# The FFN of a hybrid diffusion step in scaled float16 pairs, split once and kept in DRAM

## The chip, the cores and the metric

The kernel runs on one core of one Trainium2 chip. A core has a matrix engine (TensorE, "PE" in the profile), a vector engine (DVE), a scalar engine (ACT), a third compute engine (POOL) and an engine that only issues transfers (SP). Each has its own queue of instructions and works through it in order; semaphores tie them together. [...] Transfers between DRAM and SBUF run on 16 DMA engines, which all queues share.

The metric is the device time of one execution in microseconds (us), given as the median over several runs.

## What is computed

One layer of a backbone over 128 context tokens and 1024 latent tokens, 1152 rows in all, with a model width of 1024. Attention heads and mLSTM heads stand side by side, one output projection merges them, and an FFN follows. What matters here is the FFN:

```python
def swiglu(h, w_gu, w_down):
    g, u = jnp.split(h @ w_gu, 2, axis=-1)
    return (jax.nn.silu(g) * u) @ w_down

def trunk_layer(...):
    ...
    mix = jnp.concatenate([attn_o, hm], axis=-1) @ w_out
    x = x + g1 * mix
    h2 = rmsnorm(x, norm2_w) * (1 + sc2) + sh2
    x = x + g2 * swiglu(h2, w_gu, w_down)
    return x, ak, av, st_f, st_b
```

All tensors are float32. `w_gu` is 1024 x 5632 (gate, then up, `D_FF` = 2816 columns each), `w_down` is 2816 x 1024.

## The kernel before

**Products of pairs.** To keep the accuracy of float32, each operand is split into a high part and the rest ("hi" and "lo"), and three products are added in PSUM: hi x hi, hi x lo, lo x hi. The projections at the start (`Scaled`, `linear_tok`, `head_project`) use float16 pairs: the weights are measured first (a sum of absolute values by ACT, a maximum over partitions, `power_scale`), then scaled by a power of two. The FFN and the output projection use pairs of the type fp32r, which need no scale.

**Stages in order of time.** Modulation vectors and the first norm come first. Then the four mLSTM heads: while the projection of head h+1 runs on TensorE (`head_project`), the scan of head h (`head_mlstm`) and the rest of the modulation (`ada_rest`) are woven in by `weave` and `beside`, which hand out steps of a side job in a given ratio to steps of the main one. The query projection follows, then attention and the output projection of the first third of the rows, and then the FFN.

**FFN.** The 1152 rows are cut into three chunks of 384 (`CT`). For a chunk, `norm2` makes the normed and modulated rows, transposed, as a pair of tiles (`a_tiles`). The 22 tiles of `D_FF` (`NF`) are worked in five groups (`GROUPS`, in the last chunk `LAST`) of 4 or 5. For a tile, `gate_up` loads a piece of 1024 x 128 weights for gate and one for up, and `products` (lines 1271 to 1273) issues 3 x 8 matmuls with 384 columns into each of two PSUM banks; then tanh, two DVE steps and a split give the activations as a pair. After a group, `down` multiplies its tiles with pieces of `w_down` for each half of the output: `three_blocks` (lines 1090 to 1092) works with row block 0 and then with blocks 1 and 2, and `add_gated` (lines 1079 and 1080) adds the gated result to the residual rows. The very last group goes through `down_last` (lines 1356 to 1358). So the residual rows are read and written once per group.

**Loading weights.** `load_piece` serves both the FFN and the output projection: SP issues one load of 0.5 MB into one of two `raw` buffers (line 151), ACT casts the high part (line 152), and DVE (every third time) or POOL subtracts for the low part (line 135). High and low parts have five buffers each. Every chunk loads and splits all of `w_gu` and `w_down` again.

**What runs beside the FFN.** The attention of the next chunk is woven into the groups of the current one, with a transfer that transposes on SP for each half of the probabilities (lines 1009 and 1010); the output projection of the next chunk, `attn_out`, stands before the last group, and its `norm2` is woven into the down product of that group. `finish` writes the rows of the chunk before. The order that the engines' queues finally get is that of a scheduler, which starts from this text and the priorities given with `hot`.

**Buffers.** PSUM has four banks with the tag `mm` for all these products. The tiles with the tags `b0` to `b5` in the pool `hp` are large and shared over time: `b3` to `b5` hold the normed input during the heads; `b0` and `b1` take the key stacks when attention begins; `b2` and `b3` are the pair of tiles that the FFN reads.

## Time and profile before

| | us |
|---|---|
| median of 3 runs | 1625.24 |
| lowest and highest of them | 1623.43, 1627.29 |
| span of the profiled execution | 1626.0 |

The profile is one execution, seen by the hardware profiler. Its page gives the span from the first to the last instruction; the profiled execution has no other time of its own, and its span lies within the range of the runs. Rows of the page's parts and of the trace's views have these forms:

- Groups of instructions: line, engine, operation, output and inputs by their names in the program, shapes, count, then busy us in all and the mean of one in ns, then the idle time just before them and what ended most of it.
- Stages: start and end in us, the length, then busy us with the count of instructions for PE, weight loads (PEld), DVE, ACT and POOL, the granted clock of TensorE as a share of full speed, the mean busy share of the DMA engines, and GB/s. Asked for one line alone, the row has only the busy time of that line's engine.
- Timeline: start in us, duration in us, engine, line, operation, and in brackets the idle time before and what ended it.

Matmuls are pipelined: the duration of one row is longer than the step from one start to the next, so the pace of TensorE is read from the starts.

### The profile page before, as it was taken

The page shows a single profiled execution, that of the slowest core. Times are in us where ns is not written, and L with a number is a line of the kernel's source. Part 1 is how long each engine was busy: PE and PEld are TensorE (multiplying, and loading weights), DVE is VectorE, ACT ScalarE, POOL GpSimd, SP SyncE. Part 2 cuts the span into 40 slices and gives each one's busy share as a digit, 9 for nine tenths or more (in the row PEclk, how much of TensorE's full clock was granted, in tenths as well). Part 3 has the DMA queues.
Part 4 walks back from the last instruction along what each step waited for, and adds up shares of the span by engine and source line. Part 5 has one row for each costly group of instructions (what it writes and reads, how often), then busy time and mean ns, then how long its engine had stood idle before and what let it go on. Part 6 is the DMA issues. An engine that isn't in the chain of part 4 may idle for free. (4 is left out here: it accounts for less than half of the span.)

```text
span 1626.0 us, 23528 instructions
## 1 busy us (share of the span) xinstructions
PE 1517.4 (93%) x8688; PEld 1258.8 (77%) x8688; DVE 970.8 (60%) x2059; ACT 732.5 (45%) x1251; POOL 606.5 (37%) x387
## 2 busy tenths in 40 slices
PE   5899899899879768999999999999999999999996
PEld 2745566575557557998989899898898989899995
DVE  3843364958987665467672646777674474432445
ACT  3744252434544554545643344565562453333332
POOL 0411020404344514443435354444344444545443
PEclk8999999999999878999999999999999999999998
DMA  9355352201156855767873546777684445545441
GB/s 357 94 165 130 101 147 58 84 21 46 41 198 147 195 107 112 168 168 174 187 184 112 149 141 219 187 184 173 156 183 128 134 142 170 152 126 149 130 142 66
DMA packets 386313, 232.73 MB, mean 143 GB/s; under 512 B 169910, under 2 KB 346502, under 8 KB 386198
## 3 DMA queue, kind: packets, MB, share of 16 engines
q1 hardware_dynamic: 384342, 228.04, 52.7%
q10 hardware_dynamic: 1856, 3.19, 0.6%
q8 instruction: 68, 1.11, 0.3%
q14 instruction: 47, 0.39, 0.1%
HBM read 181.16 MB, written 11.69 MB: 119 GB/s over the span
## 5 line engine op out<-in xcount | busy, mean ns | idle before, releaser
L135 POOL TENSOR_TENSOR wlo<-raw,whi 128x1024 fp32r<-128x1024 f32 x146 | 357.8, 2454 | 445.7 <-ACT whi L152 407.9
L152 ACT CAST whi<-raw 128x1024 fp32r<-128x1024 f32 x219 | 224.4, 1025 | 375.9 <-DMA raw<-in_w_gu_dram 137.8
L1272 PE MATMUL mm<-aTl,whi 128*128 128x384 f32 (+2 forms) x1088 | 364.7, 335 | 0.7 <-POOL aTl L135 0.7
L1273 PE MATMUL mm<-aTh,wlo 128*128 128x384 f32 (+2 forms) x1088 | 364.4, 335 | 0.0
L1271 PE MATMUL mm<-aTh,whi 128*128 128x384 f32 (+2 forms) x1088 | 363.4, 336 | 0.7 <-DVE tn L1299 0.7
L1272 PEld LDWEIGHTS mm<-aTl,whi 128*128 128x128 f32 x1088 | 205.9, 189 | 1.7 <-POOL aTl L135 0.9
L1271 PEld LDWEIGHTS mm<-aTh,whi 128*128 128x128 f32 x1088 | 205.4, 189 | 2.0 <-DVE tn L1299 1.3
L1273 PEld LDWEIGHTS mm<-aTh,wlo 128*128 128x128 f32 x1088 | 205.8, 189 | 0.1
L135 DVE TENSOR_TENSOR wlo<-raw,whi 128x1024 fp32r<-128x1024 f32 (+1 forms) x73 | 88.1, 1206 | 142.2 <-ACT whi L152 141.7
L1090 PE MATMUL mm<-whi,hl 128*128 128x512 f32 x372 | 145.8, 397 | 1.5 <-ACT hl L1303 1.4
L1091 PE MATMUL mm<-wlo,hl 128*128 128x512 f32 x372 | 146.9, 397 | 0.0
L1092 PE MATMUL mm<-whi,hl 128*128 128x512 f32 x372 | 144.3, 396 | 0.7 <-POOL hl L135 0.7
L1007 DVE SCALAR_TENSOR_TENSOR pl<-pr,st,ph 128x1152 f16<-128x1152 f32 (+1 forms) x72 | 107.8, 1498 | 39.4 <-ACT ph L1006 39.4
L488 PE MATMUL wi<-ipair,hT 128*128 128x384 f16 (+2 forms) x392 | 128.2, 327 | 2.8 <-ACT ipair L216 2.8
L489 PE MATMUL wi<-ipair,hT 128*128 128x384 f16 (+2 forms) x392 | 128.1, 327 | 0.0
L490 PE MATMUL wi<-ipair,hT 128*128 128x384 f16 (+2 forms) x392 | 127.1, 326 | 0.0
L135 POOL TENSOR_TENSOR hl<-tn,hl 128x384 fp32r<-128x384 f32 x66 | 84.2, 1276 | 105.0 <-ACT hl L1303 105.0
L1003 ACT ACTIVATE pr<-S,st 128x1152 f32<-128x1152 f32 (+1 forms) x72 | 81.1, 1127 | 89.1 <-DVE st L1002 86.1
L1299 DVE SCALAR_TENSOR_TENSOR tn<-tn,mm 128x384 f32<-128x384 f32 (+2 forms) x68 | 36.7, 540 | 137.9 <-PE mm L1273 97.5
L1080 DVE TENSOR_TENSOR x<-x,t 128x512 f32<-128x512 f32 x102 | 116.5, 1163 | 0.8
L1000 PE MATMUL S<-kst,qT 128*128 128x384 f32 (+1 forms) x400 | 88.3, 355 | 19.6 <-ACT pr L1003 19.2
L1002 DVE TENSOR_REDUCE st<-S 128x1 f32<-128x1152 f32 (+1 forms) x72 | 88.9, 1234 | 18.3 <-PE S L1000 17.8
(353 smaller groups left out, 2684.6 us busy)
## 6 DMA issues: line engine op xcount, KB each, us to landing
raw<-in_w_gu_dram SPq DMA_DIRECT2D x132, 512.0 KB
raw<-in_w_down_dram SPq DMA_DIRECT2D x60, 512.0 KB
a<-in_w_ada_dram SPq DMA_DIRECT2D x32, 512.0 KB
gl<-g_d SPq DMA_DIRECT2D x36, 256.0 KB
aw<-in_w_ada_dram SPq DMA_DIRECT2D x16, 512.0 KB
iraw<-in_w_in_dram SPq DMA_DIRECT2D x32, 256.0 KB
raw<-in_w_out_dram SPq DMA_DIRECT2D x15, 512.0 KB
x<-in_x_sample_dram SPq DMA_DIRECT2D x13, 512.0 KB
```

The source lines that it names most:

```text
L135: (dve if eng == "dve" else pool).tensor_tensor(out=out, in0=full, in1=hi, op=ALU.subtract)
L152: nc.scalar.copy(hi[:, :n], raw[:, :n])
L488: mm(ps[:, :n], ah, wh[:, k % 2, c0 : c0 + n], start=(k == 0), stop=False)
L489: mm(ps[:, :n], ah, wl[:, k % 2, c0 : c0 + n], start=False, stop=False)
L490: mm(ps[:, :n], al, wh[:, k % 2, c0 : c0 + n], start=False, stop=(k == KD - 1))
L1080: eng.tensor_tensor(out=x1[:, cs], in0=x1[:, cs], in1=t, op=ALU.add)
L1090: mm(ps, ah, wh[:, k % 2, :], start=(k == 0), stop=False)
L1091: mm(ps, ah, wl[:, k % 2, :], start=False, stop=False)
L1092: mm(ps, al, wh[:, k % 2, :], start=False, stop=(k == nk - 1))
L1271: mm(ps, wh[:, k, :], th[:, k, :], start=(k == 0), stop=False)
L1272: mm(ps, wh[:, k, :], tl[:, k, :], start=False, stop=False)
L1273: mm(ps, wl[:, k, :], th[:, k, :], start=False, stop=(k == KD - 1))
```

## The change

The FFN's operands become float16 pairs with scales, and the weights are split only in the first chunk. In parts:

1. **Measurement of weights** (`measure`). Beside heads 1 to 3 and the query projection, all of `w_gu` and `w_down` is loaded in 33 units of 1 MB into buffers with the tags `b0` to `b2`. ACT squares them with a column sum into `sq`, for 55 tiles of weights. One matmul with ones adds over the partitions, and DVE makes a power-of-two scale and its inverse for each tile (`wsc`, and `fsc` for the activations). Each load follows a small POOL copy that reads a tile which the heads have just made.
2. **Bound on the normed rows** (`bound_h2`). From the modulation vectors, a power-of-two scale that is put into them.
3. **Pairs** (`split_pair`, `gu_piece`, `down_piece`). In chunk 0 a piece is loaded, scaled and split: on odd turns with one ACT and one DVE step, on even turns with two ACT steps and one on POOL. The pair is one tile and is written to DRAM (`gu_d`, `wd_d`). In chunks 1 and 2 a piece is one load of that pair. The pairs take buffers of either of the two old tags in turn, ten in all.
4. **Activations.** `gate_up` keeps them in float32 in one of 20 slots; ACT takes a sum of absolute values of each tile. When a group is done, `rescale` finds the maximum of these sums, makes a power of two, and scales and splits the group's tiles. The inverse scale goes into `add_gated`.
5. **Groups.** Two in a chunk (12 and 10 tiles), three in the last (10, 8 and 4). `down` holds three PSUM banks, one for each row block, and uses each piece for all three. The down product of a group stands behind the first three tiles of the next one (for the short last group, behind all of it); that of the last group stands behind the output projection of the next chunk, and `norm2` is woven into it.
6. **Normed rows.** The pair is one float16 tile, `b2` or `b3` in turn.

```diff
-GROUPS = [(0, 4), (4, 4), (8, 4), (12, 5), (17, 5)]
-LAST = [(0, 5), (5, 5), (10, 4), (14, 4), (18, 4)]
+GROUPS = [(0, 12), (12, 10)]
+LAST = [(0, 10), (10, 8), (18, 4)]
...
+    def measure(after):
...
+        def load(u):
+            src, a, _ = srcs[u]
+            t = hp.tile([P, 3072], F32, name=nm("ms"), tag=f"b{u % 3}")
+            pool.tensor_copy(t[:, 0:1], after())
+            dma(t[:, 0:2048].rearrange("p (a n) -> p a n", a=a), src)
+            return t
...
+            if a == 2:
+                act(t[:, 0:2048], t[:, 0:2048], AF.Square, accum_out=sq[:, col : col + 1])
+            else:
+                for i in range(2):
+                    v = t[:, 0:2048].rearrange("p (k i n) -> p i k n", k=KD, i=2)[:, i]
+                    act(v, v, AF.Square, accum_out=sq[:, col + i : col + i + 1])
+            yield
...
+        mm(ps[:, 0:NS], ones, sq, start=True, stop=True)
...
-    weave(head_project(1, sts[1]), beside((scan, 1.15), (ada, 0.45)), 56, 56)
+    weave(head_project(1, sts[1]), beside((scan, 1.15), (ada, 0.45), (meas, 0.2)), 56, 56)
...
-    weave(head_project(2, sts[2]), beside((scan, 1.15), (ada, 0.55)), 56, 56)
+    weave(head_project(2, sts[2]), beside((scan, 1.15), (ada, 0.55), (meas, 0.22)), 56, 56)
...
-    weave(head_project(3, sts[3]), beside((scan, 1.15), (kwork, 0.5)), 56, 56)
+    weave(head_project(3, sts[3]), beside((scan, 1.15), (kwork, 0.5), (chain(bound_h2(), meas), 0.3)), 56, 56)
...
-    weave(linear_tok(w_q, 0, 512, ev_q, QFIRST), scan, 24, 60)
+    weave(linear_tok(w_q, 0, 512, ev_q, QFIRST), beside((scan, 1.0), (meas, 0.15)), 24, 60)
     emit(scan)
+    emit(meas)
...
+    def split_pair(src, shape, col, keep):
+
+        t, (hi, lo) = pair(shape)
+        raw = wp.tile([P, 1024], F32, name=nm("raw"), tag="raw", bufs=2)
+        dma(raw.rearrange("p (a b) -> p a b", b=shape[1]), src)
+        sc = wsc[:, 0, col : col + 1]
+        lo_count[0] += 1
+        if lo_count[0] % 2:
+            act(t[:, 0], raw, AF.Copy, scale=sc)
+            dve.scalar_tensor_tensor(out=t[:, 1], in0=raw, scalar=sc, in1=t[:, 0], op0=ALU.mult, op1=ALU.subtract)
+        else:
+            act(raw, raw, AF.Copy, scale=sc)
+            nc.scalar.copy(t[:, 0], raw)
+            sub(t[:, 1], raw, t[:, 0], "pool")
+        dma(keep, t)
+        return hi, lo
...
-                act(tn[:, cs], g, AF.Tanh, scale=0.5)
+                act(tn[:, cs], gp_, AF.Tanh, scale=fsc[:, 0, f : f + 1])
...
+            jk = ft.tile([P, D], BF16, name=nm("jk"), tag="t2", bufs=3)
+            act(jk[:, 0:CT], tn, AF.Abs, accum_out=g["st"][:, i : i + 1])
...
+        for i, tn in enumerate(g["a"]):
+            hl = hlp.tile([P, 2, CT], F16, name=nm("hl"), tag="hl", bufs=SLOTS)
+            act(hl[:, 0], tn, AF.Copy, scale=m[:, 1:2])
+            dve.scalar_tensor_tensor(out=hl[:, 1], in0=tn, scalar=m[:, 1:2], in1=hl[:, 0], op0=ALU.mult, op1=ALU.subtract)
+            g["hl"].append(hl)
...
+    def down(c, a, g):
+        for n in range(2):
+            gate = gate_bc(1, c, n)
+            banks = [bank() for _ in range(CB)]
+            for j in range(0, g["nf"], 2):
+                w = down_piece(c, (g["f0"] + j) // 2, n)
+                for i, ps in enumerate(banks):
+                    down_products(ps, g, j, i, w)
+                    if j + 2 == g["nf"]:
+                        add_gated(a["x1"][i], ps, gate(c * CB + i), n, inv=g["inv"])
+                    yield 2
...
-    nc = _bacc.Bacc("TRN2", target_bir_lowering=False, num_devices=1)
+    nc = _bacc.Bacc("TRN2", target_bir_lowering=False, num_devices=1, dynamic_dma_scratch_size=1024)
```

[...]

More of the change, by code (lines that the diff above doesn't have):

```diff
@@ L1301, in gate_up @@
[L1301 to L1317 removed]
+                dve.scalar_tensor_tensor(out=tn[:, cs], in0=tn[:, cs], scalar=fsc[:, 1, f : f + 1], in1=gp_, op0=ALU.mult, op1=ALU.mult)
@@ L1332, in finish, with down_last @@
             yield
-    def down_last(c, a, f0, nf):
+    def down_last(c, a, g):
         gs, ws = [], []
@@ L1444, in hybrid_step @@
         else:
-            main = groups(c, cur, LAST[:-1])
+            grps = [new_group(*x) for x in LAST]
+            main = groups(c, cur, grps)
             for _ in range(4):
```

264 lines of the change are left out of this document (183 added, 81 removed).

## The prediction

> **What bounds the kernel now.** I read the page's first two parts first: how busy each engine is, and how that is spread over forty slices of the span.
>
> ```profile
> PE 1517.4 (93%) x8688; PEld 1258.8 (77%) x8688; DVE 970.8 (60%) x2059; ACT 732.5 (45%) x1251; POOL 606.5 (37%) x387
> PEclk8999999999999878999999999999999999999998
> ```
>
> TensorE is busy nearly everywhere, but the page warns that a busy PE is not a PE at its peak, so I went on to the table of stages: columns are PE, weight loads, DVE, ACT, POOL, the granted clock, the DMA share and GB/s.
>
> ```profile
> 0.00:50.00 50.00, 29.33 (x152) 13.67 (x152) 24.39 (x114) 23.85 (x50) 4.19 (x9) 0.86 0.97 342
> 160.00:400.00 240.00, 226.62 (x1522) 150.97 (x1521) 152.32 (x519) 96.67 (x283) 54.27 (x79) 0.98 0.30 76
> 400.00:450.00 50.00, 41.47 (x224) 25.21 (x225) 45.08 (x154) 25.59 (x74) 16.39 (x18) 0.93 0.18 63
> 660.00:850.00 190.00, 188.13 (x1086) 171.35 (x1086) 128.70 (x176) 101.86 (x133) 77.04 (x37) 1.00 0.77 179
> 850.00:985.00 135.00, 135.00 (x704) 123.58 (x703) 63.58 (x103) 51.82 (x70) 62.49 (x32) 1.00 0.47 138
> 985.00:1340.00 355.00, 350.99 (x1943) 320.51 (x1942) 232.42 (x336) 177.78 (x239) 152.10 (x71) 1.00 0.65 167
> 1395.00:1605.00 210.00, 210.00 (x1112) 196.99 (x1112) 80.76 (x94) 66.01 (x84) 99.26 (x51) 1.00 0.45 132
> ```
>
> The rows are: start; mLSTM heads 0 to 3; query projection; chunk 0 with attention beside it; chunk 0 after attention; chunk 1; chunk 2. From 660 us on, PE is idle for 1.9, 0, 4.0 and 0 us, at a clock of 1.00. Whether the busy time is full pace shows in the timeline, between the starts of the first and last row of an unbroken run. The FFN's products first, 384 then 512 columns wide:
>
> ```profile
> 1404.77 0.34 PE L1272 MATMUL mm<-aTl,whi 128*128 128x384 f32 x1
> 1411.88 0.34 PE L1271 MATMUL mm<-aTh,whi 128*128 128x384 f32 x1
> ...
> 1395.76 0.39 PE L1091 MATMUL mm<-wlo,hl 128*128 128x512 f32 x1
> 1399.96 0.39 PE L1091 MATMUL mm<-wlo,hl 128*128 128x512 f32 x1
> ```
>
> The first pair has 41 steps between it: 7.11/41 = 0.1734 us a product. The second has 18: 4.20/18 = 0.2333 us. So the FFN is bound by how many products PE must stream and at what pace. A loader, a wait or an engine that gets cheaper there gives nothing; only the pace does.
>
> **What the change takes away.** The projections before it already use float16 pairs, with the same tiles; their runs give the new pace.
>
> ```profile
> 171.99 0.33 PE L490 MATMUL wi<-ipair,hT 128*128 128x384 f16 x1
> 173.94 0.33 PE L490 MATMUL wi<-ipair,hT 128*128 128x384 f16 x1
> ...
> 439.96 0.38 PE L489 MATMUL mm<-ipair,hT 128*128 128x512 f16 x1
> 444.06 0.38 PE L490 MATMUL mm<-ipair,hT 128*128 128x512 f16 x1
> ```
>
> 12 steps in 1.95 us are 0.1625 us; 19 steps in 4.10 us are 0.2158 us. The counts come from the groups of instructions by form; each of these lines has two sisters with the same count.
>
> ```profile
> L1272 PE MATMUL mm<-aTl,whi 128*128 128x384 f32 x1024 | 345.8, 338 | 0.0
> L1091 PE MATMUL mm<-wlo,hl 128*128 128x512 f32 x372 | 146.9, 397 | 0.0
> L1357 PE MATMUL mm<-wlo,hl 128*128 128x512 f32 x24 | 9.5, 394 | 0.0
> ```
>
> Gate and up: 3 x 1024 = 3072 products x (0.1734 - 0.1625) = 33.5 us. Down: 3 x (372 + 24) = 1188 x (0.2333 - 0.2158) = 20.8 us. Together **-54.3 us**. Regrouping changes no product count. The 192 narrower products of the first two tiles I leave at nothing, either way.
>
> [...]
>
> **What it adds: the measurement beside the heads.** 33 loads of 1 MB, 44 ACT squares of 1024 columns and 11 of 2048, in the stage from 160 to 450 us. Nearest rows for ACT, with the rows of the splitting steps that I need below:
>
> ```profile
> L199 ACT ACTIVATE jk<-iraw 128x1024 bf16<-128x1024 f32 x20 | 21.2, 1058 | 7.6 <-DMA iraw<-in_w_in_dram 7.3 <-issue 0.3
> L199 ACT ACTIVATION_READ_ACCUMULATOR jk<-iraw 128x1 f32 x20 | 3.9, 193 | 0.0
> L216 ACT ACTIVATE ipair<-iraw,isc 128x1024 f16<-128x1024 f32 x10 | 11.5, 1152 | 1.9 <-PE wi L490 1.8
> L219 ACT ACTIVATE iraw<-iraw,isc 128x1024 f32<-128x1024 f32 x10 | 10.9, 1140 | 2.1 <-DVE isc L204 2.1
> L220 ACT CAST ipair<-iraw 128x1024 f16<-128x1024 f32 x10 | 10.4, 1041 | 0.0
> L152 ACT CAST whi<-raw 128x1024 fp32r<-128x1024 f32 x207 | 217.0, 1049 | 348.4 <-DMA raw<-in_w_gu_dram 137.8 <-PE mm L1272 58.4 <-DMA raw<-in_w_down_dram 48.1
> L1303 ACT CAST hl<-tn 128x384 fp32r<-128x384 f32 x66 | 33.7, 510 | 34.2 <-DVE tn L1300 34.0
> ```
>
> 44 x 1.25 + 11 x about 2.2 = 79 us of ACT. ACT has 122 of 290 us there now; it would have 201. Its queue is in order: behind each square wait the head's evacuations, its exponentials and so the matmuls that read them, while PE has only 22 us of slack (290 less 226.62 and 41.47). The loads fit: 34.6 MB at the 342 GB/s of the first row is 101 us, against a share of 0.30 used. But each load is issued by SP behind a small POOL copy that waits for a fresh block of the head, and the next head's weights queue behind it on SP.
>
> No row has a square of this size in this place, so bounds. Below: 0, since nothing of that stage is removed. Above: if the whole stage fell from 94% busy PE (226.62/240) to the 83% of the row from 400 to 450 us (41.47/50), where ACT and DVE are crowded, 290 x 0.11 = 32 us. DVE is not loaded more here, so I take less than half: **+14 us**. The tail of it (one matmul over the column sums, some ten small DVE steps, the bound on h2) is inside that.
>
> **Chunk 0: splitting and keeping.** 66 pieces are loaded, split and also written to DRAM; 4 are needed before 660 us. Besides the ACT rows above:
>
> ```profile
> L135 DVE TENSOR_TENSOR wlo<-raw,whi 128x1024 fp32r<-128x1024 f32 x67 | 83.9, 1252 | 118.0 <-ACT whi L152 117.6 <-issue 0.4
> L217 DVE SCALAR_TENSOR_TENSOR ipair<-iraw,isc,ipair 128x1024 f16<-128x1024 f32 x10 | 16.0, 1612 | 8.6 <-ACT ipair L216 8.6
> L135 POOL TENSOR_TENSOR wlo<-raw,whi 128x1024 fp32r<-128x1024 f32 x140 | 350.1, 2504 | 435.7 <-ACT whi L152 397.8 <-issue 10.8 <-DVE t L1079 8.4
> L135 POOL TENSOR_TENSOR ipair<-iraw,ipair 128x1024 f16<-128x1024 f32 x10 | 23.4, 2348 | 64.7 <-ACT ipair L220 64.7
> ```
>
> A split took 1.05 + 2.50 us (two of three, POOL) or 1.05 + 1.25 us (DVE). Now an odd piece takes 1.15 + 1.61 = 2.8 us, an even one 1.14 + 1.04 + 2.35 = 4.5 us; mean 3.65 against 3.13. The two raw buffers are held from issue to end of split. The landing shows between an issue by SP and the cast that waited for it, quiet and beside attention:
>
> ```profile
> 1404.70 0.37 SPq L151 DMA_DIRECT2D raw<-in_w_gu_dram  x1
> 1409.29 1.05 ACT L152 CAST whi<-raw 128x1024 fp32r<-128x1024 f32 x1 [2.05 <-DMA raw<-in_w_gu_dram]
> ...
> 1001.13 0.81 SPq L151 DMA_DIRECT2D raw<-in_w_gu_dram  x1
> 1007.97 1.05 ACT L152 CAST whi<-raw 128x1024 fp32r<-128x1024 f32 x1 [4.14 <-DMA raw<-in_w_gu_dram]
> ```
>
> Quiet: 4.2 us; beside attention 6.0 us. With 0.4 us of hand-overs the loader makes a piece every (4.2 + 3.65 + 0.4)/2 = 4.1 us, where PE now takes 24 x 0.1625 = 3.9 us for one. Beside attention the write of another piece lies ahead of it, 1.5 us (0.52 MB at 342/0.97 GB/s, first row of the stages): (7.5 + 4.05)/2 = 5.8 us.
>
> How many pieces each stretch split before:
>
> ```profile
> 660.00:850.00 190.00, 38.42 (x37) 1.00 0.77 179
> 850.00:985.00 135.00, 32.94 (x33) 1.00 0.47 138
> ```
>
> That is a piece every 5.1 and 4.1 us. The 70 include four of the output projection and the first of chunk 1; chunk 1 now splits nothing, and ten pieces instead of five may be ready ahead, so some 59 remain: 33 x 5.8 + 26 x 4.1 = 298 us, against 325 - 18 = 307 us that PE needs. The loader just keeps up. DMA is tighter: 0.77 x 190 = 146 us of full work in the first stretch and 33 writes x 1.5 = 50 us more make 196 us, for a stretch that PE would end in about 180: 16 us over, part of which may move into the second stretch (0.47 x 135 = 63 us used). Bounds: 0, if the traffic spreads; 45 us, if a piece takes the loader 1 us more than reckoned in the first stretch (33 us) and nothing is caught up in the second (12 us). Nothing here can gain. I take **+12 us**, near the DMA sum.
>
> [...]
>
> **Groups, rescaling, chunks 1 and 2.** Seven groups instead of fifteen. Each now waits for its own maximum (two PE steps, seven small DVE steps) before 4 to 12 tiles are scaled: ACT 0.51 us each, DVE about 0.6 us (1612 ns x 384/1024), so about 12 us to the last tile. Behind it waits the group's down product; ahead of it in PE's order lie three tiles of the next group (6 x 3.9 = 23 us) or the output projection of the next chunk (72 products x 0.2333 = 17 us). Bounds: 0, and 7 x 2 us where attention delays it. I take **+2 us**. Fewer groups save DVE and POOL work, off PE's path: nothing. In chunks 1 and 2 a piece is one 0.5 MB load without a split; of the 4.0 us of idle PE in chunk 1 and some near its end I let **3 us** go. What is late next there is PE itself.
>
> The sum, against the execution's own span: 1626.0 - 54.3 + 14 + 12 + 2 - 3 = 1596.7. The span is 0.8 us above the median of the runs, 1625.24, so **1596 us**.
>
> **Rivals.**
> - All additions hide: 1626 - 54 - 3 - 1 = 1568. For it: ACT and DMA are half free in the heads, and ten pieces of stock. Against: PE there waits for ACT already.
> - The heads pay in full, 32 instead of 14: 1614, and with 25 us in chunk 0 about 1627, no change.
> - Slower: chunk 0 becomes bound by its DMA. Transposes, writes and reads share SP's queue; if a landing beside attention reaches 11 us, a piece takes (11 + 4.05)/2 = 7.5 us: 33 x 7.5 + 26 x 4.5 = 365 us for PE's 307, 58 in place of 12, so 1642. It decides from 41 us in chunk 0 on (54 + 3 - 14 - 2), a mean of 5.9 us a piece. For it: share 0.77 already. Against: quiet second stretch.
> - The pace does not change, since f32 products as wide were not bound by their type: 1626 + 14 + 12 + 2 - 4 = 1650. The float16 runs speak against it.
> - Products overlap further than the runs show, until the float16 weight load is the bound, at 0.10 us:
>
> ```profile
> L489 PEld LDWEIGHTS <-hT 128*128 128x128 f16 x432 | 43.2, 100 | 31.0 <-issue 8.2
> ```
>
>   then down alone gives 1188 x (0.2333 - 0.10) = 158 us for 21, so 1459. The same runs speak against it, since they have this weight load and step at 0.2158 us. [...]
>
> **Chances.** Mine (1580 to 1618) 0.50; all hidden (1565 to 1580) 0.23; heads in full 0.11 (half of it no change); chunk 0 on DMA 0.13; pace unchanged 0.02; further overlap 0.01. Range 1568 to 1634: it leaves out the worse half of the slower case, the fast edge and the two small ones. A measurement of this kernel tells about 0.2%, 3.3 us, from no change: faster 0.80, same 0.05, slower 0.15.
>
> **What would show it.** Starts of float16 FFN products 0.1625 and 0.2158 us apart; chunk 2, from first gate product to last down product, about 18 us shorter; the heads' stage some 14 us longer with ACT near 70%; PE waits in chunk 0 that lead back to DMA of raw pieces; none in chunk 1. Wrong if the heads grow by over 32 us, chunk 0 by over 40, or a rescale leaves PE idle for more than 2 us.

## The result, and the profile after

The changed kernel takes 1679.74 us (median of 4 runs, 1679.43 to 1680.37) beside 1626.26 us before (4 runs, 1623.43 to 1628.04): a ratio of 1.034, 95% interval 1.0321 to 1.0359. It is slower, where 1596 us and faster were forecast. The profiled execution spans 1677.6 us, 51.6 more than before. The first row of its page:

```profile
PE 1499.1 (89%) x8714; PEld 935.7 (56%) x8714; DVE 871.6 (52%) x2065; ACT 745.6 (44%) x1388; POOL 265.0 (16%) x252
```

TensorE is busy for 18 us less and yet the span is longer: idle time grew by 70 us. Where it lies is seen from the starts of four products in the timeline: the first of the output projection (the heads and query projection are over), and the first gate product of chunks 0, 1 and 2. They divide the spans of all runs of this study as follows (us; the last column runs to the end of the span). The stages are those of one profiled execution each, and the runs of one kernel lie up to 15 us apart (h_ungated), so single differences of a few us carry little weight.

| kernel | time (ratio to before) | span | heads | up to chunk 0 | chunk 0 | chunk 1 | chunk 2 |
|---|---|---|---|---|---|---|---|
| before | 1626.26 | 1626.0 | 457.8 | 622.1 | 361.5 | 351.4 | 291.0 |
| after | 1679.74 (1.034) | 1677.6 | 510.3 | 671.6 | 401.3 | 332.9 | 271.7 |
| h_none | 1619.13 (0.9975) | 1621.4 | 458.8 | 624.1 | 394.4 | 331.4 | 271.5 |
| h_loads | 1633.17 (1.0062) | 1633.2 | 475.4 | 629.9 | 400.0 | 331.8 | 271.4 |
| h_squares | 1648.18 (1.0163) | 1646.1 | 478.4 | 635.5 | 406.9 | 332.3 | 271.4 |
| h_ungated | 1639.46 (1.0098) | 1639.9 | 478.3 | 648.0 | 388.1 | 332.4 | 271.4 |
| h_free | 1638.60 (1.0098) | 1638.3 | 472.2 | 642.6 | 392.1 | 332.3 | 271.2 |
| h_va | 1640.59 (1.0104) | 1637.5 | 482.8 | 643.9 | 390.9 | 331.2 | 271.5 |
| h_kt3 | 1668.15 (1.027) | 1667.0 | 500.1 | 662.1 | 402.0 | 331.3 | 271.6 |
| h_so | 1663.29 (1.0239) | 1660.2 | 492.4 | 659.5 | 397.6 | 331.7 | 271.5 |
| c_late | 1658.01 (1.0204) | 1653.7 | 505.7 | 668.1 | 383.1 | 331.3 | 271.3 |
| c_raw3 | 1653.00 (1.0173) | 1649.6 | 502.9 | 670.9 | 373.4 | 333.2 | 272.1 |
| c_odd | 1646.67 (1.0134) | 1639.4 | 505.5 | 664.6 | 371.5 | 332.0 | 271.4 |
| c_alias | 1642.37 (1.0107) | 1639.6 | 507.0 | 664.8 | 372.1 | 331.0 | 271.7 |
| c_noload | 1606.30 (0.9895) | 1607.5 | 510.6 | 669.7 | 334.9 | 331.7 | 271.3 |
| c_all | 1633.68 (1.0063) | 1634.0 | 504.6 | 670.0 | 359.5 | 333.0 | 271.4 |
| c_all_nostore | 1627.89 (1.0022) | 1620.7 | 506.5 | 669.5 | 347.2 | 332.3 | 271.7 |
| g_best | 1609.01 (0.991) | 1604.5 | 484.1 | 640.4 | 357.8 | 335.1 | 271.2 |
| g_va | 1609.83 (0.9906) | 1611.3 | 486.3 | 644.6 | 362.2 | 333.2 | 271.2 |

After against before: 49.5 us more up to chunk 0, 39.8 more in it, 18.5 and 19.3 less in chunks 1 and 2. With the forecast pace chunk 0 too should have been 18.1 us shorter, so its loss is 57.9. The gain came in full; about twice its size, 49.5 + 57.9 us, was lost in the two places where the change adds work. The table of stages of after (columns as in the prediction) shows what those two have in common:

```profile
150.00:510.00 360.00, 304.21 (x1860) 193.91 (x1857) 207.12 (x730) 191.11 (x480) 82.73 (x131) 0.93 0.60 164
...
671.60:1072.90 401.30, 353.15 (x2029) 220.66 (x2029) 211.31 (x331) 215.54 (x297) 80.20 (x38) 0.94 0.80 220
1073.00:1406.00 333.00, 328.78 (x1928) 204.47 (x1927) 169.19 (x307) 127.06 (x209) 7.05 (x3) 1.00 0.66 172
1406.00:1650.00 244.00, 244.00 (x1395) 136.31 (x1393) 63.48 (x131) 40.38 (x94) 0.00 (x0) 1.00 0.41 136
```

The same heads, and chunk 0, in before:

```profile
150.00:458.00 308.00, 285.41 (x1855) 185.76 (x1854) 208.80 (x705) 128.60 (x369) 74.91 (x99) 0.97 0.29 77
...
622.10:983.60 361.50, 357.00 (x2024) 326.33 (x2022) 212.79 (x319) 172.47 (x230) 152.56 (x75) 0.99 0.63 158
```

For nearly the same number of products TensorE is idle 55.8 us instead of 22.6 in the heads, and busy 19 us longer, at a granted clock of 0.93 instead of 0.97. So 33 us of the 52 are waits, and 19 are longer busy time; the ratio of the two clocks gives some 12 of these 19 (285.41 x 0.97/0.93 - 285.41), the rest stays open. In chunk 0, 48.2 us are idle instead of 4.5, at a granted clock of 0.94 instead of 0.99. Chunks 1 and 2 run at 1.00, chunk 2 without a gap. The starts of the FFN's products there, 39 steps apart in the first pair of rows and 19 in the second:

```profile
1409.78 0.33 PE L1383 MATMUL mm<-h,wpair 128*128 128x384 f16 x1
...
1416.12 0.33 PE L1383 MATMUL mm<-h,wpair 128*128 128x384 f16 x1
...
1617.38 0.38 PE L1449 MATMUL mm<-wpair,hl 128*128 128x512 f16 x1
...
1621.48 0.38 PE L1450 MATMUL mm<-wpair,hl 128*128 128x512 f16 x1
```

6.34/39 = 0.1626 and 4.10/19 = 0.2158 us: the pace is the one forecast.

### The profile page after: what moved, and what is told of

It reads as the page before. It is cut to its first block, busy times and chain, and to the rows that moved or that the text cites. A ratio compares the mean times of both kernels' runs of the same rounds, so it can differ in the third digit from the quotient of the medians.

```text
span 1677.6 us, 23385 instructions
## 1 busy us (share of the span) xinstructions
PE 1499.1 (89%) x8714; PEld 935.7 (56%) x8714; DVE 871.6 (52%) x2065; ACT 745.6 (44%) x1388; POOL 265.0 (16%) x252
## 5 line engine op out<-in xcount | busy, mean ns | idle before, releaser
L1383 PE MATMUL mm<-h,wpair 128*128 128x384 f16 (+2 forms) x1088 | 349.9, 323 | 4.8 <-DVE tn L1414 3.2
L1384 PE MATMUL mm<-h,wpair 128*128 128x384 f16 (+2 forms) x1088 | 350.4, 323 | 0.5 <-POOL h L137 0.5
L1385 PE MATMUL mm<-h,wpair 128*128 128x384 f16 (+2 forms) x1088 | 350.6, 323 | 0.0
L1449 PE MATMUL mm<-wpair,hl 128*128 128x512 f16 x396 | 149.9, 381 | 1.6 <-DVE tn L1413 1.6
L1450 PE MATMUL mm<-wpair,hl 128*128 128x512 f16 x396 | 150.7, 381 | 0.0
L1451 PE MATMUL mm<-wpair,hl 128*128 128x512 f16 x396 | 149.6, 380 | 0.0
L1384 PEld LDWEIGHTS <-wpair 128*128 128x128 f16 x1088 | 107.3, 99 | 71.1 <-issue 6.8
L1385 PEld LDWEIGHTS <-wpair 128*128 128x128 f16 x1088 | 107.2, 99 | 69.6 <-issue 4.9
L1383 PEld LDWEIGHTS <-wpair 128*128 128x128 f16 x1088 | 107.0, 99 | 67.5 <-issue 2.6
L1088 DVE SCALAR_TENSOR_TENSOR pl<-pr,st,ph 128x1152 f16<-128x1152 f32 (+1 forms) x72 | 103.6, 1441 | 52.8 <-ACT ph L1087 52.8
L1081 PE MATMUL S<-kst,qT 128*128 128x384 f32 (+1 forms) x400 | 98.4, 383 | 34.5 <-ACT pr L1084 27.1
L137 POOL TENSOR_TENSOR wpair<-raw,wpair 128x1024 f16<-128x1024 f32 x33 | 72.7, 2202 | 308.0 <-ACT wpair L1342 287.5
L1416 ACT ACTIVATE jk<-tn 128x384 bf16<-128x384 f32 x66 | 34.4, 521 | 158.9 <-DVE tn L1414 111.7
L1081 PEld LDWEIGHTS S<-kst,qT 128*128 128x128 f32 x400 | 76.7, 209 | 45.3 <-ACT pr L1084 34.3
L1087 ACT ACTIVATE ph<-pr,st 128x1152 f16<-128x1152 f32 (+1 forms) x72 | 83.4, 1159 | 30.3 <-issue 11.3
L1105 PE MATMUL po<-phT,vs 128*128 128x256 f16 x292 | 76.8, 294 | 20.6 <-DMA phT<-ph 14.8
```

What stands on the lines that cost most here:

```text
L1081: mm(S[:, n, 0:w], qT[:, h, :], kst[kv][:, t, c0 + n * w : c0 + (n + 1) * w], start=(t == 0), stop=(t == 1))
L1088: dve.scalar_tensor_tensor(out=plv, in0=prv, scalar=st[:, 3:4], in1=phv, op0=ALU.mult, op1=ALU.subtract)
L1383: mm(ps, wh[:, k, :], th[:, k, :], start=(k == 0), stop=False)
L1384: mm(ps, wh[:, k, :], tl[:, k, :], start=False, stop=False)
L1385: mm(ps, wl[:, k, :], th[:, k, :], start=False, stop=(k == KD - 1))
L1449: mm(ps, ah, wh[:, k], start=(j + k == 0), stop=False)
```

## The experiments on the heads

Some names first. SyncE and GpSimd are SP and POOL of the profile. An evacuation copies finished products out of PSUM; ScalarE evacuates a block of a head into `kt`, VectorE into `va`. `dt` and `sd` are later steps of the scan. The gate is the small GpSimd copy ahead of each load of the measurement.

Theory A says that squares at the head of ScalarE's in-order queue wait for loads that were issued late. Its rivals are the traffic of the loads, or SyncE held behind the gates (theory B), and the plain time of the squares on ScalarE (theory C). Theory A came from two views of after. The waits of the heads, ScalarE's first and then TensorE's longest (who waited, for what: us in all, times, longest):

```profile
ACT ms L539 <- DMA ms<-in_w_gu_dram: 61.9, 17, 19.8
ACT ms L535 <- DMA ms<-in_w_down_dram: 31.4, 6, 9.6
...
PE mm L909 <- DVE sd L887: 17.9, 6, 9.9
```

The squares wait 93 us for their loads, at the head of ScalarE's queue. The timeline shows why the loads are late:

```profile
272.03 0.30 POOL L524 COPY ms<-kt 128x1 f32<-128x1 f32 x2 [16.38 <-ACT kt L801]
272.24 0.39 SPq L525 DMA_DIRECT2D ms<-in_w_down_dram  x1
...
283.42 1.91 ACT L535 ACTIVATE ms<-ms 128x2048 f32<-128x2048 f32 x1 [7.22 <-DMA ms<-in_w_down_dram]
...
285.33 0.35 ACT L801 ACTIVATE kt<-wi,isc 128x128 f32<-128x128 f32 x1
285.79 0.18 POOL L524 COPY ms<-kt 128x1 f32<-128x1 f32 x1 [13.46 <-ACT kt L801]
...
289.72 1.12 ACT L885 ACTIVATE dt<-mm,QT 128x128 f32<-128x128 f32 x4
...
290.35 0.94 DVE L887 TENSOR_TENSOR sd<-mm,dt 128x256 f32<-128x256 f32 x2 [9.96 <-ACT dt L885]
290.83 1.23 PE L909 MATMUL mm<-va,sd 128*128 128x129 f32 x4 [9.94 <-DVE sd L887]
```

A square at 283.42 had waited 7.22 us for its load. Behind it stood the evacuation of kt (285.33), for which the gate copy had waited 13.46 us, and behind the gate stands the next load. It is a loop: square, evacuation, gate, load, square. The head's `dt` (289.72) stands in the same queue, and TensorE ends up waiting 9.94 us.

**h_none**: the measurement is left out; the norms are a constant.

```diff
-        ahead = [load(0), load(1)]
...
+        dve.memset(sq, 1.0)
```

> The measurement's loads, its POOL copies and its squares are left out; the column sums are set to 1, so the scales are constants instead of measured ones. The heads' stage (up to the first product of the output projection) took 457.8 us before the change and 510.3 us after. Every theory: with all of it gone the stage ends near 458 to 462, the total near 1679 - 50 = 1630. If the stage stays above 475, the growth is not the measurement's at all.

1619.13 us, ratio 0.9975 (0.9955 to 0.9994). Up to chunk 0 it takes 624.1 us, 2.0 more than before: the 47.5 us above that are the measurement's. Chunk 0 keeps 394.4 us, so most of its loss has another cause.

**h_loads**: loads and gate copies as in after, the squares left out, the norms a constant.

```diff
-            if a == 2:
-                act(t[:, 0:2048], t[:, 0:2048], AF.Square, accum_out=sq[:, col : col + 1])
...
+        dve.memset(sq, 1.0)
```

> The 33 loads of 1 MB and their POOL copies stay, the 55 squares are left out (column sums set to 1). Theory A (a square stands at the head of ACT's queue and waits for a load that was issued late, and the heads' evacuations wait behind it): the stage ends within 10 us of the kernel without any measurement, total near 1632. Theory B (the loads' traffic, or SP held behind the POOL copies): the stage stays near 500, total near 1670.

1633.17 us, ratio 1.0062 (1.0039 to 1.0085). The time is theory A's. The heads, 475.4 us, are 16.6 over h_none and not within 10, but far from theory B's 500; up to chunk 0 it is 629.9, 5.8 over h_none, so part of the work seems only to have moved across the boundary.

**h_squares**: the same 55 squares, on three tiles that are loaded once; 30 loads are left out. The squares write their output to the unused end of the tile, as bfloat16, so that the three tiles stay as loaded.

```diff
-            dma(t[:, 0:2048].rearrange("p (a n) -> p a n", a=a), src)
+            if u < 3:
+                dma(t[:, 0:2048].rearrange("p (a n) -> p a n", a=a), src)
```

> The 55 squares stay, but read three tiles that are loaded once; 30 of the 33 loads are left out, so the scales are wrong. Theory A (waiting on late loads): the stage grows by 5 to 15 us over the kernel without measurement, total near 1640. Theory C (79 us of ACT time in a queue that is nearly the bound): it grows by 40 us or more, total near 1672.

1648.18 us, ratio 1.0163 (1.0131 to 1.0195). The heads grow by 19.6 us over h_none, between theory A's 5 to 15 and theory C's 40; up to chunk 0 it is 635.5 us, 11.4 over h_none. Loads alone and squares alone make 17 us there; together they cost 47.5. By the whole times the sum is less far off: 14.0 and 29.1 us alone, 60.6 together. Some 17 to 30 us exist only when a square can wait for a load, which fits the loop.

**h_ungated**: the gate copy alone is left out.

```diff
-            pool.tensor_copy(t[:, 0:1], after())
```

> All of the measurement stays, only the POOL copy ahead of each load goes, so that a load is issued as soon as its buffer is free. Theory A: squares find their data landed; the stage ends near 475, total near 1645. Theories B and C: no change, total 1675 to 1682.

1639.46 us, ratio 1.0098 (1.0038 to 1.0158): 40 us below after, as theory A expected; B and C expected no change. The heads fall by 32 us to 478.3; up to chunk 0 it is 24 us.

**h_free**: loads without gates and without squares, the norms a constant.

```diff
-            pool.tensor_copy(t[:, 0:1], after())
...
-                act(t[:, 0:2048], t[:, 0:2048], AF.Square, accum_out=sq[:, col : col + 1])
...
+        dve.memset(sq, 1.0)
```

> Left out: the squares and the GpSimd copies that gate the measurement's loads (the loads all run, the norms are a constant). Theory A (the cost of the measurement's loads is the order they impose: SyncE's queue and GpSimd wait at each gate): without gates the loads cost nothing, heads 457 to 462 us, time 1616 to 1624 us, about that of the run without any measurement; the 20 us that the ungated run still had are then the squares in ScalarE. Rival D (30 transfers of 1 MB slow the heads' own transfers): heads 470 to 478 us, as in the run with gated loads, time 1630 to 1640 us.

1638.60 us, ratio 1.0098 (1.0078 to 1.0119); heads 472.2, 18.5 us over h_none up to chunk 0. My theory that loads without gates cost nothing fell; the time and the heads are those of the rival, that the loads slow the heads' own transfers. Two rows of its stages and two of its waits:

```profile
50.00:100.00 50.00, 46.37 (x362) 33.46 (x363) 39.34 (x113) 33.83 (x70) 22.82 (x25) 1.00 1.08 349
...
150.00:200.00 50.00, 37.65 (x246) 24.70 (x244) 14.02 (x49) 10.09 (x25) 0.11 (x2) 0.80 1.08 273
```

```profile
PE mm L853 <- DVE cs L863: 9.2, 1, 9.2
...
DVE cs L863 <- DMA cs<-in_state_n_dram: 8.5, 1, 8.5
```

Without a gate the DMA share is 1.08 from 50 to 100 and from 150 to 200 us; in h_none it is 0.36 from 150 to 200 us. In that second stretch a small load, a head's old state, keeps VectorE waiting for 8.5 us, and TensorE stands still for 9.2 us, about half of the 18.5. So loads alone are cheaper with a gate: 5.8 us up to chunk 0 against 18.5, and 14.0 against 19.5 by the whole times. With the squares in place that advantage does not show: no gate (h_ungated, 1639.46) and a better gate (h_va below, 1640.59) are level.

**h_va**: the gate stays, but copies a word of `va`, which VectorE evacuates, instead of `kt`, which ScalarE does.

```diff
-        return done_b[-1][1][:, 0:1] if done_b else st["q"][0][:, 0:1]
+        return done_b[-1][2][:, 0:1] if done_b else st["q"][0][:, 0:1]
```

> The gate stays on GpSimd and paces the loads as before, but copies a word of va, which VectorE evacuates, in place of kt, which ScalarE evacuates. Theory A (a loop: the square waits for its load, the load for the gate, the gate for an evacuation queued behind the square in ScalarE): the loop is cut, heads 470 to 482 us in place of 510, time 1638 to 1650 us. Rival (a GpSimd gate ahead of each load costs it wherever its word comes from, since GpSimd and SyncE run in order): heads 495 to 512 us, time 1665 to 1680 us. Below 470 us it would also show that paced loads cost less than the early ones of the ungated run.

1640.59 us, ratio 1.0104 (1.0086 to 1.0122); heads 482.8. One index takes off 39 us. ScalarE's waits for the loads, 93.3 us in after, are now:

```profile
ACT ms L539 <- DMA ms<-in_w_gu_dram: 29.9, 15, 8.3
...
ACT ms L535 <- DMA ms<-in_w_down_dram: 12.2, 4, 9.6
```

All loads, squares and GpSimd copies are still there, so a rival by which any GpSimd gate costs this falls. Of the 40.1 us by which the span shrinks, 27.7 lie up to chunk 0 and 10.4 in chunk 0. But one doubt was left: the scheduler lays every kernel's queues anew, and here it also put the squares further back in ScalarE's queue. Two more gates were meant to tell the loop from that.

**h_kt3**: the gate copies `kt` of two blocks earlier; a word that is older, but still ScalarE's.

```diff
-        return done_b[-1][1][:, 0:1] if done_b else st["q"][0][:, 0:1]
+        return done_b[-3:][0][1][:, 0:1] if done_b else st["q"][0][:, 0:1]
```

> The gate copies a word of the kt two blocks older than in the changed kernel, so it asks for nothing that is still to be evacuated soon. Theory A in its strict form (any word that ScalarE makes closes the loop, since the scheduler puts the square as close behind its gate as before: 10 ScalarE instructions on the mean in both kernels): heads 495 to 512 us, time 1665 to 1682 us. Rival P (what counts is only how old the word is, not which engine makes it): heads 475 to 485 us, time 1638 to 1648 us, as with va.

1668.15 us, ratio 1.027 (1.0243 to 1.0296); heads 500.1: within what theory A expected. An older word helps by 12 us, far from va's 39.

**h_so**: the gate copies a word of `so`, which VectorE makes out of `th`, an evacuation of ScalarE.

```diff
-        return done_b[-1][1][:, 0:1] if done_b else st["q"][0][:, 0:1]
+        return done_b[-1][3][:, 0:1] if done_b else st["q"][0][:, 0:1]
```

> The gate copies a word of so, which VectorE makes, but from th, which ScalarE evacuates behind kt: the loop through ScalarE stays, one step longer. Theory A: heads 495 to 515 us, time 1660 to 1685 us. Rival P' (it is enough that the word is VectorE's, or that the scheduler then puts the squares further back, 19 ScalarE instructions behind the block's kt instead of 10, and 31 with va): heads 478 to 492 us, time 1640 to 1655 us.

1663.29 us, ratio 1.0239 (1.021 to 1.0267). The time is within theory A's range, the heads, 492.4, fall just between the two. ScalarE's waits for the loads here:

```profile
ACT ms L539 <- DMA ms<-in_w_gu_dram: 30.5, 17, 5.3
...
ACT ms L535 <- DMA ms<-in_w_down_dram: 21.9, 6, 8.5
```

By the whole times 23 of va's 39 us come back, of which 9.6 lie in the heads. By the sum of ScalarE's waits for loads the kernels stand in the order of their heads: after 93.3 us and 510.3, h_kt3 74.8 and 500.1, h_so 52.4 and 492.4, h_va 42.1 and 482.8.

How long the gate itself waited for its word shows how far the loop was closed. GpSimd's waits in after, h_kt3, h_so and h_va:

```profile
POOL ms L524 <- ACT kt L801: 62.1, 5, 18.1
...
POOL ms L524 <- ACT kt L801: 63.3, 7, 22.4
...
POOL ms L524 <- DVE so L808: 9.2, 13, 2.9
...
POOL ms L524 <- DVE va L803: 3.3, 2, 2.1
```

With a word of ScalarE the gate waits 62 and 63 us, the older word no less; with one of VectorE 9 us or less. That is theory A's link, and it is cut in h_so too: what still sets h_so apart from h_va is not a gate that waits for its word, and these runs do not show what it is. The doubt is not settled either: in the traces, 11 ScalarE instructions on the mean lie between the last evacuation of `kt` ahead of a gate and the square behind it in after and h_kt3, and 21 to 22 in h_so and h_va (reads of the accumulator not counted). The engine of the word and the place of the squares changed together.

## The experiments on chunk 0

Here too the theory (D) came from a timeline of after, at SyncE's queue, ScalarE and GpSimd:

```profile
776.53 1.57 SPq L1334 DMA_DIRECT2D raw<-in_w_gu_dram  x2
...
783.06 1.15 ACT L1341 ACTIVATE raw<-raw,wsc 128x1024 f32<-128x1024 f32 x1 [3.09 <-DMA raw<-in_w_gu_dram]
785.41 2.13 POOL L137 TENSOR_TENSOR wpair<-raw,wpair 128x1024 f16<-128x1024 f32 x1 [12.19 <-ACT wpair L1342]
787.57 1.42 SPq L1344 DMA_DIRECT2D gu_d<-wpair  x2
789.08 1.68 SPq L1334 DMA_DIRECT2D raw<-in_w_gu_dram  x2
```

Two raw pieces are issued together, land together, are split, stored, and only then does SyncE reach the next two loads. Landing and splitting do not overlap: 12.55 us for two pieces, 6.3 us each. The waits of SyncE in chunk 0 name the queue:

```profile
SPq L1344 <- POOL wpair L137: 99.4, 25, 8.5
SPq L1344 <- DVE wpair L1339: 23.7, 13, 6.8
```

For 123 of the 401 us SyncE stands before a store whose pair is not split, with the next load behind it. One rival (theory E) is the bandwidth: a share of 0.80, with the writes. Another (theory F) is that two raw buffers are too few for the longer split, wherever the stores stand.

How a late piece reaches TensorE is not seen in SyncE's queue. No wait of an FFN product is put down to a split pair in after; TensorE's longest waits in chunk 0 stand before attention, and ScalarE waits for raw pieces:

```profile
PE S L1081 <- ACT pr L1084: 10.6, 8, 2.8
...
PE S L1081 <- DVE qT L137: 7.1, 2, 4.2
...
ACT raw L1341 <- DMA raw<-in_w_gu_dram: 66.7, 18, 6.7
```

With the other three such rows, ScalarE waits 113.6 us for raw pieces in chunk 0. One of TensorE's gaps, row by row:

```profile
757.13 1.15 ACT L1341 ACTIVATE raw<-raw,wsc 128x1024 f32<-128x1024 f32 x1 [5.65 <-DMA raw<-in_w_gu_dram]
...
759.26 0.57 ACT L1059 CAST qT<-mm 64x512 fp32r<-64x512 f32 x1
...
760.61 0.69 PE L1081 MATMUL S<-kst,qT 128*128 128x384 f32 x1 [4.17 <-DVE qT L137]
```

The split waits 5.65 us for its piece, the cast of attention's `qT` stands behind it in ScalarE's queue, and TensorE waits 4.17 us for `qT`. So this is the delay of the heads once more: a step that waits for a load at the head of an in-order queue, with the steps of other work behind it. That all of the idle time comes in this way is not shown.

**c_late**: the store is issued behind the load of the next piece but one.

```diff
+        if len(unkept) > 1:
+            dma(*unkept.pop(0))
...
-        dma(keep, t)
+        unkept.append((keep, t))
```

> Same work; only the place of the stores of finished pairs on SP's queue moves: the store of a pair is issued behind the load of the piece after next. Chunk 0 (first gate product to that of chunk 1) took 361.5 us before the change, 401.3 after; TensorE alone would need about 343. Theory D (loads queue on SP behind stores that wait for splits, so that load and split no longer overlap): chunk 0 takes 345 to 370 us, total near 1640. Theory E (34.6 MB of stores fill the DMA engines): no change, 395 or more. Theory F (two raw buffers with a longer split): no change, 395 or more.

1658.01 us, ratio 1.0204 (1.0125 to 1.0282); chunk 0 falls by 18 us to 383.1, with the same bytes: a smaller gain than theory D's 345 to 370 and a larger one than E and F allow. SyncE now waits 77 us (57.3 for splits on GpSimd, 19.4 on VectorE) before the loads themselves, until a split frees one of the two raw buffers.

**c_alias**: 62 of the 66 stores are left out (the expectations say 63), and chunks 1 and 2 read the first stored pairs.

```diff
-        dma(keep, t)
+        if col in (0, NF, 2 * NF):
+            dma(keep, t)
...
-        keep = gu_d[f][:, j].rearrange("p h k n -> p h (k n)")
+        keep = gu_d[0][:, j].rearrange("p h k n -> p h (k n)")
```

> Only the pairs of the first tile of gate, up and down are stored, and chunks 1 and 2 read these for every piece: 63 of 66 stores are left out, so the output is wrong from chunk 1 on. Theories D and E: chunk 0 takes 345 to 365 us, total near 1635. Theory F: chunk 0 stays above 385.

1642.37 us, ratio 1.0107 (1.0037 to 1.0177); chunk 0 372.1 us, between what D and E (up to 365) and F (above 385) expected.

**c_raw3**: a third raw buffer (the kernel that ran had 17 `hl` buffers to make room).

```diff
-        raw = wp.tile([P, 1024], F32, name=nm("raw"), tag="raw", bufs=2)
+        raw = wp.tile([P, 1024], F32, name=nm("raw"), tag="raw", bufs=3)
...
-SLOTS = 20
+SLOTS = 17
```

> Three raw buffers instead of two (18 activation slots instead of 20 pay for the space). Theory F: chunk 0 takes 350 to 370 us. Theory D: little, 385 to 400, since the loads still stand behind the stores. Theory E: no change.

1653.00 us, ratio 1.0173 (1.01 to 1.0246); chunk 0 373.4 us: near theory F's 350 to 370, and below theory D's 385 to 400.

**c_odd**: every piece is split with one ScalarE and one VectorE step, none on GpSimd.

```diff
-        if lo_count[0] % 2:
+        if True:
```

> Every piece is split with one ACT and one DVE step (2.8 us reckoned), none with two ACT steps and one on POOL (4.5 us reckoned). Theory F: chunk 0 falls to about 375 us. Theory D: a little less too, since stores wait for shorter splits, 385 or so. Theory E: no change, 395 or more.

1646.67 us, ratio 1.0134 (1.0031 to 1.0237); chunk 0 371.5 us, near theory F's 375 and below theory D's 385. This and c_alias decide against the bandwidth as the main cause. Chunk 0 in c_odd:

```profile
664.60:1036.10 371.50, 342.89 (x2030) 214.27 (x2030) 235.10 (x362) 188.10 (x269) 17.17 (x10) 0.98 0.88 239
```

and in c_alias:

```profile
664.80:1036.90 372.10, 344.54 (x2030) 215.82 (x2030) 206.10 (x331) 216.03 (x298) 84.59 (x40) 0.96 0.61 155
```

The same length at a DMA share of 0.88 and of 0.61, both 30 us below after's at 0.80. Each way of shortening the loop of load, split and store that was run helps, with or without the bytes. Neither theory D nor F holds alone: the place of the stores is worth 18 us, a third buffer 28 and a shorter split 30. ScalarE's waits alone do not order the kernels: in c_odd it still waits 101 us for raw pieces.

**c_noload**: after the first piece of each matrix there are no raw loads, splits and stores; later pieces of all chunks read the first stored pair.

```diff
-        if c == 0:
+        if c == 0 and f == 0:
...
-        keep = gu_d[f][:, j].rearrange("p h k n -> p h (k n)")
+        keep = gu_d[0][:, 0].rearrange("p h k n -> p h (k n)")
```

> Left out: after the first piece of each matrix, the raw loads, the splits and the stores of chunk 0; every later piece of all three chunks reads the first stored pair, so the output is not the reference's. Theory L (the loop load, split, store of the raw pieces delays chunk 0): the chunk falls from 401 us to 343 to 352 us, what the faster pace alone leaves of 361.5, and the time to about 1625 to 1633 us. Rival C (chunk 0 is long for another reason: the granted clock, or its other work beside the FFN): 370 us or more remain, as in the runs that shortened the loop, and the time stays at 1640 us or above.

1606.30 us, ratio 0.9895 (0.9871 to 0.9918). Chunk 0:

```profile
669.70:1004.60 334.90, 332.30 (x2030) 211.34 (x2030) 162.04 (x302) 123.48 (x206) 9.59 (x6) 1.00 0.65 170
```

334.9 us at full clock, 2.6 us idle, below the 343 that the theory expected; rival C falls, and the whole excess is the loader's. Against after it is 66.4 us: 45.6 of idle TensorE, and 20.9 in which the same products took longer at a clock of 0.94.

**c_all**: c_raw3, c_late and c_odd together.

```diff
-        raw = wp.tile([P, 1024], F32, name=nm("raw"), tag="raw", bufs=2)
+        raw = wp.tile([P, 1024], F32, name=nm("raw"), tag="raw", bufs=3)
...
-        if lo_count[0] % 2:
+        if True:
...
-        dma(keep, t)
+        unkept.append((keep, t))
```

> The three shortenings of the loop together: a third raw buffer, stores issued behind the next load, no POOL step. Theory L with gains that add up in part: chunk 0 at 350 to 362 us, time 1625 to 1635 us. Rival: each of the three takes away the same one delay, and what is left is something else: 368 to 374 us again, time 1636 to 1645 us. The heads stay at 505 us.

1633.68 us, ratio 1.0063 (1.004 to 1.0086). Chunk 0 takes 359.5 us, 41.8 less than after. The single gains were 27.9, 18.2 and 29.8, so they add up only in part.

**c_all_nostore**: c_raw3 and c_odd with c_alias's left-out stores in place of c_late.

```diff
-        raw = wp.tile([P, 1024], F32, name=nm("raw"), tag="raw", bufs=2)
+        raw = wp.tile([P, 1024], F32, name=nm("raw"), tag="raw", bufs=3)
...
-        if lo_count[0] % 2:
+        if True:
...
-        dma(keep, t)
+        if col in (0, NF, 2 * NF):
+            dma(keep, t)
```

> The third raw buffer and the splits without GpSimd, and in place of the later issue of the stores, 63 of the 66 stores left out (chunks 1 and 2 read the first stored pair; the output is not the reference's). It takes apart the 25 us that chunk 0 still stood above the run that neither loads nor splits. If they are the stores (traffic of 33 MB beside the raw loads, pair buffers held until a store lands): 336 to 345 us, time 1608 to 1618 us. If they are the splits on ScalarE and VectorE (or raw loads) in the way of the chunk's other work: 353 to 360 us, time 1626 to 1634 us.

1627.89 us, ratio 1.0022 (1.0009 to 1.0036); chunk 0 in the profile 347.2 us:

```profile
669.50:1016.70 347.20, 334.79 (x2029) 213.17 (x2029) 233.81 (x362) 187.26 (x267) 13.99 (x8) 0.99 0.64 165
```

Chunk 0 lies between the two expectations, the time within that of the splits. By the profiles the stores are 12.3 of the last 24.6 us and the splits and raw loads 12.3; by the medians it is 5.8 and 21.6. Both take part; how much each is not settled.

## Both places mended

**g_best**: c_all and the gate copy left out as in h_ungated.

```diff
-            pool.tensor_copy(t[:, 0:1], after())
```

> The loop shortened as in the run before, and the gate copy of the measurement left out as in the run without it. If the two delays are independent, as the theory of two separate causes says: heads 478 us, chunk 0 as in the run before, time 35 to 40 us under that run, 1588 to 1600 us, faster than both kernels. If one hides behind the other (measuring that moves out of the heads meets the loader in chunk 0): 1605 to 1625 us.

1609.01 us, ratio 0.991 (0.9887 to 0.9933): 0.9% faster than before, but 16 us above c_all less h_ungated's 40. The table says where most of this lies: of those 40 us, 13 had lain in chunk 0 (401.3 to 388.1), and with the shortened loop only 2 are left to take there (359.5 to 357.8). The two delays are not independent.

**g_va**: c_all with the gate on `va`.

```diff
-        return done_b[-1][1][:, 0:1] if done_b else st["q"][0][:, 0:1]
+        return done_b[-1][2][:, 0:1] if done_b else st["q"][0][:, 0:1]
```

> The gate on va, with chunk 0's loop shortened in the three ways. Theory A and two separate causes: heads as in the run before, chunk 0 at 355 to 362 us, time 1595 to 1612 us, level with the run that drops the gate (1609.0). Rival as before: heads near 505 us, 1630 to 1636 us, as the shortened loop alone.

1609.83 us, ratio 0.9906 (0.9885 to 0.9927), level with g_best and within theory A's range.

## Why the prediction was wrong

- **Pace, -54.3 us: right.** Chunks 1 and 2 are 18.5 and 19.3 us shorter, where the pace was to give 18.1 each, and c_noload's chunk 0 is 26.6 shorter than before's. Of the 8.5 us beyond the pace, 1.9 are idle time (4.5 against 2.6); the rest may be before's own splitting and its clock of 0.99, which no run takes apart.
- **Idle regained -3, rescaling +2: too small to decide, and not borne out one by one.** Chunk 1 has 4.2 us of idle TensorE (333.00 - 328.78) where before had 4.0, so nothing was regained there; chunk 2 shows 244.00 busy us of 244. In chunk 0 of after one rescale did stop TensorE for more than the 2 us that I had set as a sign of error:

```profile
1008.05 0.37 PE L116 MATMUL mm<-ident,gm 128*1 128x128 f32 x1 [4.56 <-DVE gm L1425]
```

  c_noload has the same rescales and 2.6 us of idle in all of chunk 0, so this gap too goes with the loader.
- **Heads, +14 with an upper bound of 32: the failed step.** The squares' work was priced well: 79 us of ScalarE were forecast, and it had 77.8, of which 10.6 went to reading the sums:

```profile
L539 ACT ACTIVATE ms<-ms 128x1024 f32<-128x1024 f32 x44 | 46.2, 1054 | 61.9 <-DMA ms<-in_w_gu_dram 61.9
L535 ACT ACTIVATE ms<-ms 128x2048 f32<-128x2048 f32 x11 | 21.0, 1910 | 31.4 <-DMA ms<-in_w_down_dram 31.4
```

  What was not priced is the 93.3 us of waits in front of them. I wrote that each load is issued behind a GpSimd copy "that waits for a fresh block of the head", and that ScalarE's queue is in order, but did not put the two together: the block's evacuation stands in the queue that the load's reader blocks. ScalarE was not crowded, as the +14 and its bound of 32 assumed: it was busy for 191.11 of 360 us, 53% where 70% was forecast, and stood waiting. With the gate on `va` the measurement costs 20 us up to chunk 0 (h_va, 643.9 against 624.1), inside the bounds. The bound, taken from a stage at 83% busy, was used up by the idle time alone (33 us); that busy time would itself grow, by 19 us, was in no term.
- **Chunk 0, +12 with an upper bound of 45: failed too.** The step is "a piece every (4.2 + 3.65 + 0.4)/2 = 4.1 us". It halves the sum because one raw buffer was to land while the other is split. In the trace the two go in step, since on SyncE a store that waits for its split stands ahead of the next loads; I had weighed the stores' bytes, not their place in the queue. It came to 6.3 us a piece, above the 5.9 from which my slower rival was to decide, and to 66.4 us over c_noload. The place of the stores is one link of this only: moving them gave 18 us, and then the two buffers held the loads back. The second step that failed is the comparison behind it, pieces made against pieces that TensorE needs: TensorE lost most of its idle time before attention's products, in the gap shown above because their steps stood behind a split that waited for its piece on ScalarE. This wait, 113.6 us of ScalarE, was in no term.
- **The slower rival had the size, not the mechanism.** It asked for landings of 11 us on full DMA engines. In the rows of the loader the split of two pieces began 6.5 us after the start of their issue (5.0 after its end, as the prediction counted its 4.2 and 6.0), and c_odd is shorter at a higher share (371.5 us at 0.88, after 401.3 at 0.80). I had put the writes at 16 us; with the loop shortened they cost 6 to 12 (c_all against c_all_nostore), while leaving them out of the unshortened loop took off 29.
- **The chances** rested on both additions being priced by the work they add. Both turned out to be delays of order in a queue, and both came at once.

What stays open: chunk 0 varies from 388 to 407 us in kernels with the same loader and different heads. The scheduler lays the queues anew in each; whether that makes the difference was not tried.

## What to carry to other kernels

When a copy holds back a load, follow the copied word to the engine that makes it: if the load's reader sits in that engine's in-order queue, the two can wait for each other's turn, and a word of another engine can cut the loop: `va` for `kt` took off 39 us (1679.74 to 1640.59), `so`, VectorE's too, only 16 (1663.29). Ask of every step that waits for a load which other work stands behind it in its engine's queue; that work is late too. In chunk 0 of after, where no FFN product waited for a split pair, a wait of 5.65 us for a raw piece on ScalarE ended in one of 4.17 us on TensorE. On a queue that issues loads and stores, count a store as waiting for its data, 123 us in chunk 0 here, and ask which load stands behind it. A stall of TensorE can cost more than its own length: in chunk 0 of after, 46 us of idle time beyond c_noload's went with 21 us of longer busy time, at a granted clock of 0.94 against 1.00.

## What the hardware showed that I had not expected

Some stalls of TensorE were followed by a lower clock, another was not. Three gaps in chunk 0 of after, each as two stretches of the table of stages, the first with the gap in it:

```profile
756.00:760.00 4.00, 0.44 (x3) 0.05 (x1) 0.13 (x1) 2.82 (x4) 0.52 (x1) 1.00 0.82 272
760.00:764.00 4.00, 3.40 (x12) 2.54 (x13) 3.45 (x4) 2.67 (x5) 1.62 (x1) 0.57 0.50 158
...
866.00:870.00 4.00, 1.08 (x6) 0.40 (x5) 2.65 (x7) 4.00 (x7) 0.63 (x1) 0.91 1.26 161
870.00:874.00 4.00, 3.39 (x18) 2.33 (x17) 3.25 (x3) 2.87 (x5) 1.49 (x1) 0.50 0.42 170
...
990.00:994.00 4.00, 0.80 (x6) 0.38 (x5) 1.75 (x2) 2.16 (x3) 0.53 (x1) 1.00 0.35 134
994.00:998.00 4.00, 4.00 (x25) 2.51 (x25) 1.17 (x2) 1.25 (x4) 1.83 (x1) 1.00 0.68 180
```

The gaps are 4.17, 2.92 and 3.20 us long. After the first two the granted clock is 0.57 and 0.50 in the 4 us of the second stretch; the third, longer than the second, leaves it at 1.00. In chunk 0, 46 us more of idle time than in c_noload went with 21 us more of busy time, which the clock explains (353.15 x 0.94 = 332.0, against 332.30 at 1.00); in the heads 33 went with 19, of which the clock explains some 12. Of the two shorter gaps, 2.92 us brought 0.50 and 3.20 us did not, so the length of a gap alone did not tell whether the clock fell; what else decides is not shown.
